# Other column offsets for the first four K tiles, the gated tiles and the down weights in a hybrid decoder layer

## The chip, the cores and the metric

The kernel runs on one core of one Trainium2 chip. Times are device microseconds (us) of one execution; a kernel's time is the median of its runs. TensorE does the matrix products, ScalarE and VectorE split and evict, GpSimd does small sums, SyncE issues the weight transfers.

## What is computed

One decoder layer on 256 tokens and 16 meta tokens, width 2048, in fp32: the input projection, sparse attention over a shared latent for half of the width, multi-scale pooling for the other half, then

```python
mix = jnp.concatenate([attn_out, pool_out], axis=-1) @ w_o[l]
h = layer_norm(ALPHA * h + mix, ln1_g[l], ln1_b[l])
z = h @ w_up                      # (272, 2048) @ (2048, 11264)
z = depthwise causal convolution of width 3 over z, plus a bias
a, g = jnp.split(z, 2, axis=-1)
f = (jax.nn.gelu(a) * g) @ w_down # (272, 5632) @ (5632, 2048)
h = layer_norm(ALPHA * h + f, ln2_g[l], ln2_b[l])
```

## The kernel before

Every fp32 number is split in two parts of type fp32r, an upper part (ScalarE, L170 for weights) and the rest (VectorE, L171), and a product of two numbers is three matmuls: upper by upper, and the two mixed ones. So one K tile (128 of the 2048 rows that are summed over) is a triple of matmuls. `product` (L268) runs 16 such triples into one PSUM bank: the first matmul of a triple stands at L275, the other two at L278. In these products a 128x128 block of weights is stationary and the activations, 256 to 272 tokens wide, are the moving operand. `hl.turned` sets the order of the last two: (upper weights, lower activations), then (lower weights, upper activations), or the other way round (turned).

The stages in order of time: the indexer's queries (8 products on `xp`, 256 tokens), keys and values, the attention's queries (8 on `xp`, 258 tokens), the pooling channels with the softmax between (8), the output projection (16 products, `output`, L704, on `mixp` and `mixa`), the first 8 up products on `fold` (260 columns), 80 up products on `hp` (258 tokens), and the down projection. The up products and the down projection alternate weight tile by weight tile (`ffn_plan`): `seven` (L862) computes 2x2 blocks with seven products; there the gated activations (`gp`, `right`) are stationary and the weights are the moving operand, 512 wide, in triples at L873 to L875. L925 to L927 and L1079 to L1081 are down products of the last two parts in the plain form.

Nothing is computed from where a tile lies, but the kernel sets it carefully. `weight_tiles` gives each weight tile 4224 words per partition; `places` (L106) returns the offset of the upper and of the lower part in it, whether the order is turned, and with `lead` and `gap` a step in columns: for `UP` the first 512 columns (the first four K tiles) lie at 12 and the others at 12 + 52. `Parts` (L87) places the two parts of an activation tile in its slot of 576 words: `first` and `first + 274`. The slots of the ring and the weight tiles are multiples of 64 words apart (576 and 4224), and the pools put both at 24 words past a multiple of 64. So an operand's place modulo 64 words is the same for every tile of its kind:

| operand (place modulo 64 words) | before | after |
|---|---|---|
| indexer queries: weights, activations | 34, 40 and 58 | the same |
| output projection, first four K tiles: weights, activations | 24, 26 and 44, turned | 34, 40 and 58, not turned |
| output projection, other K tiles | 24, 26 and 44, turned | the same |
| up on `hp`, first four K tiles | 36, 26 and 44, turned | 34, 40 and 58, not turned |
| up on `hp`, other K tiles | 24, 26 and 44, turned | the same |
| up on `fold`, first four K tiles | 36, 24 and 56, turned | 34, 40 and 58, not turned |
| up on `fold`, other K tiles | 24, 24 and 56, turned | 24, 26 and 44, turned |
| `gp` slots, upper and lower part (stationary) | 56 and 24 | 24 and 24 |
| `right`, upper and lower part | 24 and 56 | 24 and 24 |
| split down weights (moving) | 16 | 20 |
| the last part's down weights | 24 (`whl_y`: 24 and 32) | 20 |

K tiles are summed in the order of `K_PROJ`, `K_O` and `K_UP`, in which the weights also lie; the output projection alone took them in another order (`order`, L701) than they lie in. PE's instructions are a fixed list; nothing here reorders it. SyncE's queue fetches the weight tiles in the order of use, two ahead (three buffers).

Of the kernel before, what the change touches and what calls it, by code (L numbers as in the profile page):

```python
# [17 lines left out]
P = 128  # L18
D = 2048
NM = 16  # L20
S = 256
# [62 lines left out]
        return self.tile[rows, o + a:o + b]  # L84


class Parts:  # L87


# [8 lines left out]
WIDE = 288  # L98
QUERY = (10, 10 + 2048, False)
HEAD = (12, 12 + 2048, True)  # L100
OUTPUT = (0, 2048, True)
UP = (12, 12 + 2112, True, 512, 52)
DOWN = (56, 56 + 2048)


def places(n, kind):  # L106
# [4 lines left out]


K_PROJ = (1, 3, 5, 7, 9, 11, 13, 15, 0, 2, 4, 6, 8, 10, 12, 14)
K_O = (1, 3, 5, 7, 9, 10, 12, 14, 0, 2, 4, 6, 8, 11, 13, 15)
K_UP = (1, 3, 5, 7, 8, 10, 12, 15, 0, 2, 4, 6, 9, 11, 13, 14)


# [1 line left out]
def tile_layer(ctx, tc, xt, w_first, w_proj, w_uk, w_uv, w_pool, w_o, w_up, w_down, cols, rows, rel_bias, onehot, out):  # L119
# [82 lines left out]
    def emit(i):  # L202
        if i in ready:
            return
        if i == last:

            raw = wp.tile([P, 2048], F32, tag="wraw", name="wraw")
            nc.sync.dma_start(raw, stream[i])
            raws[i] = raw
            ready[i] = []  # L210
            for c in range(0, 2048, 256):
                hl = ring.tile([P, 2, 258], F32R, tag="act", name="whl_r", padded_shape=[P, 2, WIDE])
                nc.scalar.activation(hl[:, 0, :256], raw[:, c:c + 256], AF.Copy)
                nc.vector.tensor_tensor(hl[:, 1, :256], raw[:, c:c + 256], hl[:, 0, :256].bitcast(F32), op=ALU.subtract)
                ready[i].append(hl)
            return
        if i == spare:
            raw = wp.tile([P, 2048], F32, tag="wraw", name="wraw")
            hl = Split(sb.tile([P, 4160], F32R, tag="y", name="whl_y"), 0, 2056)
        else:  # L220
            raw, hl = weight_tiles((0, 2112) if i > spare else places(i, where.get(i)))
        ready[i] = hl
        if i == VALUES:

            nc.sync.dma_start(raw, stream[i])
# [42 lines left out]
    def product(ps, hl, act, lo, hi, places, ks=None, k0=0, k1=KT):  # L268

        for n in range(k0, k1):  # L270
            k = (places if ks is None else ks)[n]
            w = slice(P * places.index(k), P * places.index(k) + P)
            wh, wl = hl[:, 0, w], hl[:, 1, w]
            ah, al = act[k][:, 0, lo:hi], act[k][:, 1, lo:hi]
            nc.tensor.matmul(ps, wh, ah, start=n == 0, stop=False)  # L275
            turn = ((wl, ah), (wh, al)) if hl.turned else ((wh, al), (wl, ah))
            for i, (a, b) in enumerate(turn):
                nc.tensor.matmul(ps, a, b, start=False, stop=i == 1 and n == KT - 1)  # L278

# [328 lines left out]
    def values(h, pts, ptx):  # L608
        ps = small()
        hs = slice(h * HD, (h + 1) * HD)  # L610
        nc.tensor.matmul(ps[:, :NQ], vs[0][:, hs], ptx, start=True, stop=False)
        nc.tensor.matmul(ps[:, 2:NQ], vs[1][:, hs], pts[:, :2 * P], start=False, stop=False)  # L612
        nc.tensor.matmul(ps[:, 2 + P:NQ], vs[2][:, hs], pts[:, 2 * P:], start=False, stop=True)
        a = Parts(ring.tile([P, 2, WIDE], F32R, tag="act", name="mixa"), 2, NQ)
        nc.scalar.activation(a[:, 0, :NQ], ps[:, :NQ], AF.Copy)
        nc.vector.tensor_tensor(a[:, 1, :NQ], ps[:, :NQ], a[:, 0, :NQ].bitcast(F32), op=ALU.subtract)
        mix[h] = a
# [33 lines left out]
    def pooled(g, df, hl):  # L651
        for j in range(2):
            ps = small()
            for c in range(2):
                w = slice(256 * c + j * P, 256 * c + j * P + P)
                nc.tensor.matmul(ps[:, :NQ], hl[:, 0, w], df[:, c, 0, :], start=c == 0, stop=False)
                nc.tensor.matmul(ps[:, :NQ], hl[:, 0, w], df[:, c, 1, :], start=False, stop=False)
                nc.tensor.matmul(ps[:, :NQ], hl[:, 1, w], df[:, c, 0, :], start=False, stop=c == 1)
            m = 2 * g + j
            a = Parts(ring.tile([P, 2, WIDE], F32R, tag="act", name="mixp"), 2, NQ)  # L660
# [37 lines left out]
        lg = lg_next  # L698


    order = [14, 15, 12, 13, 10, 11, 0, 1, 2, 3, 4, 5, 6, 7, 8, 9]  # L701
    KC = 4

    def output(m):  # L704
        hl = weights()
        ps = big()
        product(ps[:, :NQ], hl, mix, 0, NQ, K_O, ks=order, k1=6 if m == 0 else KT)
        if m == 0:
            values(H - 1, *turned)
            less_token(*mean)  # L710
            product(ps[:, :NQ], hl, mix, 0, NQ, K_O, ks=order, k0=6, k1=14)
            pooled(*late)
            product(ps[:, :NQ], hl, mix, 0, NQ, K_O, ks=order, k0=14)
# [15 lines left out]
    def about_k(m):  # L729
# [57 lines left out]
    def normalise(m):  # L787
# [4 lines left out]
        a = Parts(ring.tile([P, 2, WIDE], F32R, tag="act", name="hp"), 2, NQ)  # L792
# [35 lines left out]
    held = {}  # L828

    def two_parts(a, src):  # L830
        nc.scalar.activation(a[:, 0], src, AF.Copy)
        nc.vector.tensor_tensor(a[:, 1], src, a[:, 0].bitcast(F32), op=ALU.subtract)
        return a

    def slot():
        a = fp.tile([P, 2, NE], F32R, name="gp", tag="gp", bufs=16, padded_shape=[P, 2, WIDE])
        return a[:, :, :2 * P].rearrange("p a (b c) -> p a b c", c=P)

    def forms(r, j, whole):
# [9 lines left out]
        right = ring.tile([P, 2, T], F32R, tag="act", name="right", padded_shape=[P, 2, WIDE])  # L851
        right = two_parts(right[:, :, :2 * P].rearrange("p a (b c) -> p a b c", c=P), s[:, 2:])
        if j % 2 == 0:
            held["lone"], held["other"] = slot(), slot() if whole else None
        two_parts(held["lone"][:, :, j % 2], a22)
        if whole:
            two_parts(held["other"][:, :, j % 2], a21)
# [4 lines left out]
    def seven(kind, part, c, j):  # L862
# [7 lines left out]
        for name, w in names:  # L870
            a, i = pairs[part][j][name]
            ps, w = held[name], slice(512 * w, 512 * w + 512)
            nc.tensor.matmul(ps, a[:, 0, i], hl[:, 0, w], start=j == 0, stop=False)  # L873
            nc.tensor.matmul(ps, a[:, 0, i], hl[:, 1, w], start=False, stop=False)  # L874
            nc.tensor.matmul(ps, a[:, 1, i], hl[:, 0, w], start=False, stop=j == n - 1)  # L875
# [31 lines left out]
    for item in plan:  # L907
# [3 lines left out]
        if item[0] == "down":  # L911
# [9 lines left out]
            for k in range(4 * g, 4 * g + 4):  # L921
                w = slice(512 * (k - 4 * g), 512 * (k - 4 * g) + 512)
                for i in range(2):
                    a, r = pairs[part][k // 2][f"a{i + 1}{k % 2 + 1}"]
                    nc.tensor.matmul(downs[i], a[:, 0, r], hl[:, 0, w], start=k == 0, stop=False)  # L925
                    nc.tensor.matmul(downs[i], a[:, 0, r], hl[:, 1, w], start=False, stop=False)
                    nc.tensor.matmul(downs[i], a[:, 1, r], hl[:, 0, w], start=False, stop=k == n - 1)  # L927
            if g == n // 4 - 1:
                for i in range(2):
                    yc = y2[:, i, 512 * c:512 * c + 512]  # L930
# [43 lines left out]
                continue  # L974
        gate(*both)
        if part > FAST:
            a = fp.tile([P, 2, NE], F32R, name="gp", tag="gp", bufs=16, padded_shape=[P, 2, WIDE])
            gated.append(two_parts(a[:, :, :S], both[0]))
        elif f % 2:
            todo.append((part, pair))  # L980

# [90 lines left out]
    for i in range(2):  # L1072
        t, mv = slice(i * P, (i + 1) * P), mvs[i]
        waiting = []
        for q, (a, b) in enumerate(cuts[i]):
            ps = small() if i else big()
            for j, k in enumerate(order):
                for o, wh, wl in pieces(hls[k], a, b):
                    nc.tensor.matmul(ps[:, o], gated[k][:, 0, t], wh, start=j == 0, stop=False)  # L1079
                    nc.tensor.matmul(ps[:, o], gated[k][:, 0, t], wl, start=False, stop=False)  # L1080
                    nc.tensor.matmul(ps[:, o], gated[k][:, 1, t], wh, start=False, stop=j == n - 1)  # L1081
# [91 lines left out]
```

## Time and profile before

| | |
|---|---|
| median of 3 runs | 1034.46 us (1034.37 to 1036.26) |
| the profiled execution | 1035.45 us, of which the span from the first to the last instruction is 1033.7 us |
| TensorE matmul busy | 1025.6 us, 99% of the span |
| VectorE, ScalarE, GpSimd busy | 86%, 60%, 18% |
| granted TensorE clock | 0.998 |

A row of a timeline gives the start in us, the length, the engine, the line, the operation, out<-in, the shape and how many instructions were merged. A matmul's length covers its way through the array, so neighbours overlap; what one costs is the distance to the next start. Since L275 begins every triple, the distance between two L275 starts is the price of one K tile.

### The profile page before, as it was taken

What the parts mean: (1) busy time and instruction counts of PE and PEld (TensorE: products, weight loads), DVE (VectorE), ACT (ScalarE), POOL (GpSimd) and SP (SyncE); (2) the same over time, 40 slices, a digit from 0 to 9 for tenths busy, and PEclk for the clock granted to TensorE, in tenths of its full rate; (3) what the DMA queues carried; (4) which work ended last, traced back from release to release, by engine and by line L of the source; (5) the groups of instructions that cost most, each with busy time, mean ns of one, the idle gap of its engine ahead of it and who ended that gap; (6) DMA issues with size and microseconds to landing.
All of it is one profiled execution on the core that took longest, in us unless ns stands there. A gap on an engine that the chain in (4) does not pass through costs nothing.

```text
span 1033.7 us, 19199 instructions
## 1 busy us (share of the span) xinstructions
PE 1025.6 (99%) x7644; PEld 976.8 (94%) x7644; DVE 890.8 (86%) x1401; ACT 621.1 (60%) x1000; POOL 185.4 (18%) x245
## 2 busy tenths in 40 slices
PE   9999999999999999999999999999999999999997
PEld 8999999999999999999999999999999999999986
DVE  6878668758879998998999999989999999999876
ACT  6656346645549855565666556565556565566675
POOL 1200014125430021120121101211112111120031
PEclk9999999999999999999999999999999999999999
DMA  9655643454554578978887788887978779887874
GB/s 328 243 187 210 226 154 106 145 194 168 200 196 137 194 225 242 287 281 288 291 277 266 277 296 275 269 277 266 300 264 286 270 278 288 277 276 274 289 235 142
DMA packets 59754, 250.28 MB, mean 242 GB/s; under 512 B 21734, under 2 KB 22416, under 8 KB 32656
## 3 DMA queue, kind: packets, MB, share of 16 engines
q1 hardware_dynamic: 34592, 230.42, 62.1%
q0 software_dynamic: 7888, 16.14, 8.2%
q10 hardware_dynamic: 17184, 2.49, 1.5%
q8 instruction: 60, 0.98, 0.4%
q14 instruction: 30, 0.25, 0.1%
HBM read 232.50 MB, written 2.11 MB: 227 GB/s over the span
## 4 chain that ended last, share of the span: by engine, by line
PE 94%; issue 2%; DVE 1%; DMA 1%; POOL 1%; ACT 0%; POOLq 0%; SPq 0%; DVEq 0%; ACTq 0%
PE mm L278 47%; PE mm L275 24%; PE at L873 6%; PE at L875 6%; PE at L874 6%; PE mm L349 2%; DMA wraw<-in_w_down 1%; DVE whl L171 1%; PE mm L577 0%; PE at L438 0%; PE at L612 0%; PE at L439 0%; POOL gb L992 0%; DMA wraw<-in_w_first 0%; PE at L324 0%
## 5 line engine op out<-in xcount | busy, mean ns | idle before, releaser
L171 DVE TENSOR_TENSOR whl<-wraw,whl 128x1024 fp32r<-128x1024 f32 (+1 forms) x416 | 486.5, 1204 | 37.0 <-ACT whl L170 36.0
L170 ACT ACTIVATE whl<-wraw 128x1024 fp32r<-128x1024 f32 (+1 forms) x416 | 402.7, 1015 | 99.3 <-DVE wraw L182 20.6
L278 PE MATMUL mm<-hp,whl 128*128 128x258 f32 x2560 | 459.6, 281 | 0.0
L278 PEld LDWEIGHTS mm<-hp,whl 128*128 128x128 f32 x2560 | 395.5, 189 | 3.1
L275 PE MATMUL mm<-hp,whl 128*128 128x258 f32 x1280 | 362.2, 283 | 0.0
L275 PEld LDWEIGHTS mm<-hp,whl 128*128 128x128 f32 x1280 | 240.4, 188 | 3.2
L278 PE MATMUL mm<-xp,whl 128*128 128x256 f32 (+5 forms) x768 | 140.2, 282 | 0.0
L278 PEld LDWEIGHTS mm<-xp,whl 128*128 128x128 f32 x768 | 118.7, 189 | 0.5
L275 PE MATMUL mm<-xp,whl 128*128 128x256 f32 (+5 forms) x384 | 112.0, 292 | 0.0
L808 ACT ACTIVATE z<-mm,cv 128x256 f32<-128x256 f32 x40 | 22.6, 564 | 97.7 <-PE mm L278 97.7
L845 POOL TENSOR_TENSOR forms<-za 128x128 f32<-128x128 f32 x20 | 21.2, 1062 | 307.1 <-DVE za L826 240.5
L275 PEld LDWEIGHTS mm<-xp,whl 128*128 128x128 f32 x384 | 72.2, 188 | 1.0 <-issue 0.5
L875 PE MATMUL at<-whl,gp 128*128 128x512 f32 x180 | 70.7, 394 | 0.0
L874 PE MATMUL at<-whl,gp 128*128 128x512 f32 x180 | 70.7, 394 | 0.0
L873 PE MATMUL at<-whl,gp 128*128 128x512 f32 x180 | 69.4, 395 | 0.0
L808 ACT ACTIVATE za<-mm,cv 128x256 f32<-128x256 f32 x40 | 22.6, 564 | 75.6 <-PE mm L278 67.9
L848 POOL TENSOR_TENSOR forms<-za 128x128 f32<-128x128 f32 x20 | 20.3, 1014 | 199.8 <-DVE za L826 199.8
L278 PE MATMUL mm<-fold,whl 128*128 128x260 f32 x256 | 46.3, 283 | 0.0
L278 PE MATMUL mm<-mixp,whl 128*128 128x258 f32 x256 | 45.4, 278 | 0.0
L278 PE MATMUL mm<-mixa,whl 128*128 128x258 f32 x256 | 45.2, 278 | 0.0
L875 PEld LDWEIGHTS at<-whl,gp 128*128 128x128 f32 x180 | 33.8, 188 | 8.1
L874 PEld LDWEIGHTS at<-whl,gp 128*128 128x128 f32 x180 | 33.9, 188 | 6.8
(339 smaller groups left out, 1607.8 us busy)
## 6 DMA issues: line engine op xcount, KB each, us to landing
wraw<-in_w_up SPq DMA_DIRECT2D x88, 1024.0 KB, 5.0
wraw<-in_w_down SPq DMA_DIRECT2D x80, 1024.0 KB, 6.3
wraw<-in_w_proj SPq DMA_DIRECT2D x24, 1024.0 KB, 5.4
wraw<-in_w_o SPq DMA_DIRECT2D x16, 1024.0 KB, 4.9
y<-v POOLq DMA_DIRECT2D x27, 256.0 KB, 8.5
y<-u POOLq DMA_DIRECT2D x18, 256.0 KB, 4.9
wraw<-in_w_first SPq DMA_DIRECT2D x8, 304.0 KB, 5.4
x<-in_xt SPq DMA_DIRECT2D x1, 2176.0 KB, 8.0
```

The costliest lines, as they stand in the source:

```text
L170: upper = nc.scalar.activation(hl[:, 0, c], like(raw[:, c], hl, c), AF.Copy)
L171: lower = nc.vector.tensor_tensor(hl[:, 1, c], like(raw[:, c], hl, c), hl[:, 0, c].bitcast(F32), op=ALU.subtract)
L275: nc.tensor.matmul(ps, wh, ah, start=n == 0, stop=False)
L278: nc.tensor.matmul(ps, a, b, start=False, stop=i == 1 and n == KT - 1)
L349: nc.tensor.matmul(ps[:m, :T], hl[:, t // 2, a0 + a:a0 + a + m], x_parts[k][:, t % 2, :], start=k == 0 and t == 0, stop=k == KT - 1 and t ...
L808: nc.scalar.activation(z, src[:, 2:NQ], AF.Identity, bias=col(C_B, j), scale=col(C_W, 3 * j + 2))
L845: nc.gpsimd.tensor_tensor(s[:, 0], a21, a22, op=ALU.add)
L848: nc.gpsimd.tensor_tensor(s[:, 3], a11, a21, op=ALU.subtract)
L873: nc.tensor.matmul(ps, a[:, 0, i], hl[:, 0, w], start=j == 0, stop=False)
L874: nc.tensor.matmul(ps, a[:, 0, i], hl[:, 1, w], start=False, stop=False)
L875: nc.tensor.matmul(ps, a[:, 1, i], hl[:, 0, w], start=False, stop=j == n - 1)
```

## The change

The first four K tiles of the output and up products get the places of the indexer's queries, both weights and activations, and their order is no longer turned. The output projection's weights lie in the order of use. The parts of the gated tiles lie 320 words apart instead of 288 and their pool begins 32 words later; the down weights begin 4 words later. The number of instructions and their shapes stay, but for the splits of the output projection's weights, whose 1024-column pieces are now written with a step after 512 columns in their first half, as those of the up weights are.

```diff
+def begin(k, places):
+    return 2 + 14 * (places.index(k) < 4)
...
-OUTPUT = (0, 2048, True)
-UP = (12, 12 + 2112, True, 512, 52)
-DOWN = (56, 56 + 2048)
+OUTPUT = UP = (10, 10 + 2112, True, 512, 54)
+DOWN = (60, 60 + 2048)
...
-K_O = (1, 3, 5, 7, 9, 10, 12, 14, 0, 2, 4, 6, 8, 11, 13, 15)
+K_O = (14, 15, 12, 13, 10, 11, 0, 1, 2, 3, 4, 5, 6, 7, 8, 9)
...
-            hl = Split(sb.tile([P, 4160], F32R, tag="y", name="whl_y"), 0, 2056)
+            hl = Split(sb.tile([P, 4352], F32R, tag="y", name="whl_y"), 60, 60 + 2112)
-            raw, hl = weight_tiles((0, 2112) if i > spare else places(i, where.get(i)))
+            raw, hl = weight_tiles((60, 60 + 2112) if i > spare else places(i, where.get(i)))
...
-            turn = ((wl, ah), (wh, al)) if hl.turned else ((wh, al), (wl, ah))
+            turn = ((wl, ah), (wh, al)) if hl.turned and w.start >= hl.lead else ((wh, al), (wl, ah))
...
-        a = Parts(ring.tile([P, 2, WIDE], F32R, tag="act", name="mixa"), 2, NQ)
+        a = Parts(ring.tile([P, 2, WIDE], F32R, tag="act", name="mixa"), begin(h, K_O), NQ)
...
-    order = [14, 15, 12, 13, 10, 11, 0, 1, 2, 3, 4, 5, 6, 7, 8, 9]
-        product(ps[:, :NQ], hl, mix, 0, NQ, K_O, ks=order, k1=6 if m == 0 else KT)
+        product(ps[:, :NQ], hl, mix, 0, NQ, K_O, k1=6 if m == 0 else KT)
...
-    acc = fp.tile([P, NQ], F32, name="acc", tag="acc", bufs=1, padded_shape=[P, 4 * P])
+    acc = fp.tile([P, NQ], F32, name="acc", tag="acc", bufs=1, padded_shape=[P, 4 * P + 32])
...
-        a = fp.tile([P, 2, NE], F32R, name="fold", tag="gp", bufs=16, padded_shape=[P, 2, WIDE])
+        a = Parts(fp.tile([P, 2, WIDE], F32R, name="fold", tag="gp", bufs=16), begin(m, K_UP), NE)
...
+    def halves(a):
+        flat = a.rearrange("p a b -> p (a b)")
+        return [flat[:, c:c + 2 * P].rearrange("p (b c) -> p b c", c=P) for c in (0, 2 * WIDE - 2 * P)]
+
     def slot():
-        a = fp.tile([P, 2, NE], F32R, name="gp", tag="gp", bufs=16, padded_shape=[P, 2, WIDE])
-        return a[:, :, :2 * P].rearrange("p a (b c) -> p a b c", c=P)
+        return halves(fp.tile([P, 2, WIDE], F32R, name="gp", tag="gp", bufs=16))
```

`mixp` and `hp` get `begin` in the same way, `right` and the last part's gated tiles get `halves`, and the matmuls of the down projection index the parts as `a[0]` and `a[1]`.

## Rows read from the trace of the kernel before

**Rows 1.** The page: the span, the busy engines, the chain of waits by engine
```profile
span 1033.7 us, 19199 instructions
PE 1025.6 (99%) x7644; PEld 976.8 (94%) x7644; DVE 890.8 (86%) x1401; ACT 621.1 (60%) x1000; POOL 185.4 (18%) x245
PE 94%; issue 2%; DVE 1%; DMA 1%; POOL 1%; ACT 0%; POOLq 0%; SPq 0%; DVEq 0%; ACTq 0%
```

**Rows 2.** Windows by stage: us, PE, PEld, DVE, ACT, POOL busy, PEclk, DMA share, GB/s
```profile
212.00:299.00 87.00, 87.00 (x750) 86.88 (x749) 65.53 (x79) 44.02 (x79) 36.83 (x48) 1.00 0.53 183
400.00:979.00 579.00, 579.00 (x4157) 545.50 (x4156) 531.47 (x728) 345.84 (x483) 90.35 (x106) 1.00 0.83 279
```

**Rows 3.** Groups of instructions, PE, by form: busy us, mean ns, idle before
```profile
L278 PE MATMUL mm<-hp,whl 128*128 128x258 f32 x2560 | 459.6, 281 | 0.0
L275 PE MATMUL mm<-hp,whl 128*128 128x258 f32 x1280 | 362.2, 283 | 0.0
```

**Rows 4.** Timeline, PE: an up product on hp, of the slower kind
```profile
499.81 0.28 PE L275 MATMUL mm<-hp,whl 128*128 128x258 f32 x1
...
501.24 0.28 PE L275 MATMUL mm<-hp,whl 128*128 128x258 f32 x1
...
501.59 0.29 PE L275 MATMUL mm<-hp,whl 128*128 128x258 f32 x1
...
504.89 0.29 PE L275 MATMUL mm<-hp,whl 128*128 128x258 f32 x1
```

**Rows 5.** Timeline, PE: the next up product on hp, of the faster kind
```profile
507.72 0.28 PE L275 MATMUL mm<-hp,whl 128*128 128x258 f32 x1
...
509.16 0.28 PE L275 MATMUL mm<-hp,whl 128*128 128x258 f32 x1
...
512.63 0.28 PE L275 MATMUL mm<-hp,whl 128*128 128x258 f32 x1
```

**Rows 6.** Timeline, PE: an up product on hp, of the middle kind
```profile
361.07 0.28 PE L275 MATMUL mm<-hp,whl 128*128 128x258 f32 x1
...
362.84 0.28 PE L275 MATMUL mm<-hp,whl 128*128 128x258 f32 x1
```

**Rows 7.** Timeline, PE: the output projection, two neighbouring products
```profile
260.00 0.28 PE L275 MATMUL mm<-mixp,whl 128*128 128x258 f32 x1
...
265.54 0.28 PE L275 MATMUL mm<-mixp,whl 128*128 128x258 f32 x1
```

**Rows 8.** Timeline, PE: an indexer query product, 256 tokens
```profile
46.28 0.28 PE L275 MATMUL mm<-xp,whl 128*128 128x256 f32 x1
...
48.40 0.28 PE L275 MATMUL mm<-xp,whl 128*128 128x256 f32 x1
```

**Rows 9.** Timeline, PE: an up product on fold, 260 columns
```profile
332.03 0.28 PE L275 MATMUL mm<-fold,whl 128*128 128x260 f32 x1
...
333.83 0.28 PE L275 MATMUL mm<-fold,whl 128*128 128x260 f32 x1
```

**Rows 10.** Timeline, PE: 512-wide down matmuls, weights at 16; then at 24
```profile
980.06 0.40 PE L926 MATMUL mm<-whl,gp 128*128 128x512 f32 x1
...
982.39 0.39 PE L927 MATMUL mm<-whl,gp 128*128 128x512 f32 x1
...
1003.63 0.39 PE L1079 MATMUL mm<-whl,gp 128*128 128x512 f32 x1
...
1005.01 0.40 PE L1079 MATMUL mm<-whl_y,gp 128*128 128x512 f32 x1
...
1005.48 0.40 PE L1081 MATMUL mm<-whl_y,gp 128*128 128x512 f32 x1
```

**Rows 11.** Groups by form, ACT: splits in 212 to 299 us, then in 400 to 979 us
```profile
L170 ACT ACTIVATE whl<-wraw 128x1024 fp32r<-128x1024 f32 x30 | 31.0, 1053 | 32.7 <-PE mm L278 18.5 <-issue 14.1
L170 ACT ACTIVATE whl<-wraw 128x1024 fp32r<-128x1024 f32 x249 | 251.1, 1052 | 57.7 <-DVE wraw L182 20.6 <-DMA wraw<-in_w_up 19.6 <-DVE wraw L187 12.3
```

**Rows 12.** Waits of PE, longest first, whole span: us in total, times, longest
```profile
PE at L1063 <- ACT diag L1061: 1.5, 1, 1.5
```

More of the change, by code (lines that the diff above doesn't have):

```diff
@@ L659, in pooled @@
             m = 2 * g + j
-            a = Parts(ring.tile([P, 2, WIDE], F32R, tag="act", name="mixp"), 2, NQ)
+            a = Parts(ring.tile([P, 2, WIDE], F32R, tag="act", name="mixp"), begin(8 + m, K_O), NQ)
             nc.scalar.activation(a[:, 0, :NQ], ps[:, :NQ], AF.Copy, scale=col(G_POOL, m))
@@ L710, in output @@
             less_token(*mean)
-            product(ps[:, :NQ], hl, mix, 0, NQ, K_O, ks=order, k0=6, k1=14)
+            product(ps[:, :NQ], hl, mix, 0, NQ, K_O, k0=6, k1=14)
             pooled(*late)
-            product(ps[:, :NQ], hl, mix, 0, NQ, K_O, ks=order, k0=14)
+            product(ps[:, :NQ], hl, mix, 0, NQ, K_O, k0=14)
         yd = y[:, m, Q0:]
@@ L791, in normalise @@
         nc.scalar.activation(yd, yd, AF.Identity, bias=col(LN1, 2 * m + 1), scale=col(LN1, 2 * m))
-        a = Parts(ring.tile([P, 2, WIDE], F32R, tag="act", name="hp"), 2, NQ)
+        a = Parts(ring.tile([P, 2, WIDE], F32R, tag="act", name="hp"), begin(m, K_UP), NQ)
         nc.scalar.activation(a[:, 0, :NQ], yd, AF.Copy)
@@ L830, in two_parts @@
     def two_parts(a, src):
-        nc.scalar.activation(a[:, 0], src, AF.Copy)
-        nc.vector.tensor_tensor(a[:, 1], src, a[:, 0].bitcast(F32), op=ALU.subtract)
-        return a
+        nc.scalar.activation(a[0], src, AF.Copy)
+        nc.vector.tensor_tensor(a[1], src, a[0].bitcast(F32), op=ALU.subtract)
+        return a
+    def halves(a):
+        flat = a.rearrange("p a b -> p (a b)")
+        return [flat[:, c:c + 2 * P].rearrange("p (b c) -> p b c", c=P) for c in (0, 2 * WIDE - 2 * P)]
     def slot():
-        a = fp.tile([P, 2, NE], F32R, name="gp", tag="gp", bufs=16, padded_shape=[P, 2, WIDE])
-        return a[:, :, :2 * P].rearrange("p a (b c) -> p a b c", c=P)
+        return halves(fp.tile([P, 2, WIDE], F32R, name="gp", tag="gp", bufs=16))
     def forms(r, j, whole):
@@ L850, in forms @@
         mid = two_parts(slot(), s[:, :2])
-        right = ring.tile([P, 2, T], F32R, tag="act", name="right", padded_shape=[P, 2, WIDE])
-        right = two_parts(right[:, :, :2 * P].rearrange("p a (b c) -> p a b c", c=P), s[:, 2:])
+        right = two_parts(halves(ring.tile([P, 2, WIDE], F32R, tag="act", name="right")), s[:, 2:])
         if j % 2 == 0:
             held["lone"], held["other"] = slot(), slot() if whole else None
-        two_parts(held["lone"][:, :, j % 2], a22)
+        two_parts([a[:, j % 2] for a in held["lone"]], a22)
         if whole:
-            two_parts(held["other"][:, :, j % 2], a21)
+            two_parts([a[:, j % 2] for a in held["other"]], a21)
         return {"P1": (left, 0), "P2": (left, 1), "P5": (mid, 0), "P3": (mid, 1), "P6": (right, 0),
@@ L872, in seven @@
             ps, w = held[name], slice(512 * w, 512 * w + 512)
-            nc.tensor.matmul(ps, a[:, 0, i], hl[:, 0, w], start=j == 0, stop=False)
-            nc.tensor.matmul(ps, a[:, 0, i], hl[:, 1, w], start=False, stop=False)
-            nc.tensor.matmul(ps, a[:, 1, i], hl[:, 0, w], start=False, stop=j == n - 1)
+            nc.tensor.matmul(ps, a[0][:, i], hl[:, 0, w], start=j == 0, stop=False)
+            nc.tensor.matmul(ps, a[0][:, i], hl[:, 1, w], start=False, stop=False)
+            nc.tensor.matmul(ps, a[1][:, i], hl[:, 0, w], start=False, stop=j == n - 1)
         if j < n - 1:
@@ L924, in tile_layer @@
                     a, r = pairs[part][k // 2][f"a{i + 1}{k % 2 + 1}"]
-                    nc.tensor.matmul(downs[i], a[:, 0, r], hl[:, 0, w], start=k == 0, stop=False)
-                    nc.tensor.matmul(downs[i], a[:, 0, r], hl[:, 1, w], start=False, stop=False)
-                    nc.tensor.matmul(downs[i], a[:, 1, r], hl[:, 0, w], start=False, stop=k == n - 1)
+                    nc.tensor.matmul(downs[i], a[0][:, r], hl[:, 0, w], start=k == 0, stop=False)
+                    nc.tensor.matmul(downs[i], a[0][:, r], hl[:, 1, w], start=False, stop=False)
+                    nc.tensor.matmul(downs[i], a[1][:, r], hl[:, 0, w], start=False, stop=k == n - 1)
             if g == n // 4 - 1:
@@ L976, in tile_layer @@
         if part > FAST:
-            a = fp.tile([P, 2, NE], F32R, name="gp", tag="gp", bufs=16, padded_shape=[P, 2, WIDE])
-            gated.append(two_parts(a[:, :, :S], both[0]))
+            a = slot()
+            two_parts([t.rearrange("p b c -> p (b c)") for t in a], both[0])
+            gated.append(a)
         elif f % 2:
@@ L1078, in tile_layer @@
                 for o, wh, wl in pieces(hls[k], a, b):
-                    nc.tensor.matmul(ps[:, o], gated[k][:, 0, t], wh, start=j == 0, stop=False)
-                    nc.tensor.matmul(ps[:, o], gated[k][:, 0, t], wl, start=False, stop=False)
-                    nc.tensor.matmul(ps[:, o], gated[k][:, 1, t], wh, start=False, stop=j == n - 1)
+                    nc.tensor.matmul(ps[:, o], gated[k][0][:, i], wh, start=j == 0, stop=False)
+                    nc.tensor.matmul(ps[:, o], gated[k][0][:, i], wl, start=False, stop=False)
+                    nc.tensor.matmul(ps[:, o], gated[k][1][:, i], wh, start=False, stop=j == n - 1)
             yc = y2[:, i, a:min(b, 2048)]
```

## The prediction

> **What bounds the kernel now.** I read the page first: TensorE has a matmul in the array for 1025.6 of 1033.7 us, and 94% of the chain of waits is TensorE's own work [rows 1]. The waits of PE name 1.5 us as the longest wait for another engine in the whole span [rows 12]. So the time is the sum over TensorE's list of instructions of what each costs, and a change that leaves the list alone can only act through that price. A busy share of 99% does not say that the price is the lowest: a matmul's length of 281 to 283 ns is its way through the array [rows 3], and the price is the distance to the next start, which only the timeline gives. The granted clock is 1.00 in the stages of rows 2, the level of 2.4 GHz; 258 columns are 0.1075 us at that clock, three of them 0.3225 us.
>
> Now the reader should compare equal work. The output projection does one K tile in 5.54/16 = 0.346 us [rows 7]. An up product on hp has the same shapes, and in its last twelve K tiles the same places modulo 64 words and the same order. Yet one such product goes on at (504.89 - 501.59)/9 = 0.367 us per K tile [rows 4], the next at (512.63 - 509.16)/10 = 0.347 [rows 5], and a third kind at 1.77/5 = 0.354 [rows 6]. By the starts at L275 in the timeline, 38 of the 80 products on hp keep the pace of rows 4 to their end, 39 that of rows 5 and 3 that of rows 6; from 400 us on slow and fast alternate without exception. The fast and the slow product run the same instructions on operands at the same places. What differs is how they enter: their first four K tiles take about the same time (501.24 - 499.81 = 1.43 us against 509.16 - 507.72 = 1.44), but with another spacing inside, and after them a pace is fixed. So the pace depends on the places and on the moment at which a series begins; the first four K tiles are a run-up. That the output products, whose sixteen K tiles all have one place, are fast throughout fits: nothing disturbs them.
>
> **The change part by part**, summed against the profiled execution (1035.45 us, 1.0 above the median of 1034.46); I apply the differences to the median.
>
> 1. *Up products on hp.* No instruction is added. The run-up gets the places and order of the indexer's queries. Their pace is (48.40 - 46.28)/6 = 0.353 us per K tile with 256 tokens [rows 8]; two more columns in three matmuls add 0.0025 at 2.4 GHz: 0.356, so four cost 1.42 us, as now (1.43, 1.44): 0. What counts is the pace afterwards. Between the two products the 14 K tiles from the first start to the last shown take 5.08 and 4.91 us, a difference of 0.17, and two more tiles add 2 x 0.02: 0.21 us per product [rows 4, 5]. Bounds: all 38 products at 0.367 go to 0.347, -38 x 0.21 = -8.0, and the three middle ones -3 x 12 x 0.007 = -0.25; or all 39 at 0.347 go to 0.367, +8.2, with +0.45 for the middle ones. No row shows the new run-up with 258 columns in front of these places. The queries repeat one spacing from tile to tile, which speaks for one and the same moment at the end of every run-up. But with 256 columns, not 258. I take half of the gain, -4.0: slow and fast alternate now, so that there are two ways of entering, and one of them may come to hit the fast pace every time while the other goes on missing it every other time.
>
> 2. *Output projection.* Now always fast [rows 7]. The run-up at 0.356 instead of 0.346 costs 4 x 0.01 x 16 = +0.6 us. What follows can lose the fast pace: 12 x 0.0205 = 0.245 per product, 3.9 us for all sixteen. It cannot gain, for no row is below 0.346. I take four of the sixteen products at 0.367: +1.0.
>
> 3. *Up products on fold.* Now 1.80/5 = 0.360 per K tile with 260 columns [rows 9]. Their places become those of hp. With the fast pace, 4 x 0.3585 + 12 x 0.3495 = 5.63 us against 5.76, -0.13 x 8 = -1.1; with the slow one +0.9. I take -0.5.
>
> 4. *Down projection.* 756 matmuls at L873 to L875 and 96 at L925 to L927, all 512 wide, at (982.39 - 980.06)/10 = 0.233 us [rows 10]. The weights go from 16 to 20 and the stationary parts, now at 56 and 24, both to 24. Nearest rows: weights at 24 cost (1005.01 - 1003.63)/6 = 0.230, the tile after them 0.47/2 = 0.235 [rows 10]. So between -852 x 0.003 = -2.6 and +852 x 0.002 = +1.7; I take -0.6, a quarter of the gain, since the ends are about as far from the present price on either side and the row nearest in its places is the lower one.
>
> 5. *Splits.* Their count stays. The output projection's are now written with a step, as the up weights already are: 1053 ns for ScalarE in the output stage and 1052 among the up and down products [rows 11]: 0. Slots begin later by some words, no buffer is added and no transfer or queue is moved; 0. The cover is VectorE: between 400 and 979 us it is busy 531.5 of 579 us [rows 2]. If PE saved all 8 us there, VectorE would still have 40 us to spare, so the splits stay hidden; beyond that they would bound.
>
> 6. *The order of the output weights.* The same K tiles in the same order, now from the first half of a weight tile onwards. The first tiles need only the first split; the stage shows no PE idle (87.00 of 87.00 us, [rows 2]): 0.
>
> Sum: -4.0 - 0.1 + 0.6 + 1.0 - 0.5 - 0.6 = **-3.6 us, 1030.9 us**.
>
> **A rule against this change.** The timeline shows 0.347 and 0.367 us for the same triple [rows 4, 5]. The Trainium skill, "TensorE: Matmul & The Clock Gate", back-to-back issue gap, gives N / 2.4 + 2.5 ns, an estimate of 0.330 us per triple of 258 columns wherever the operands lie; and under "What happens when you issue a matmul" it says that loading the next weights does not steal read bandwidth from the running matmul. By that every place costs the same and the kernel stays at 1034.5 us. This trace does not agree: three paces for one shape, all above the estimate.
>
> **The rivals.**
>
> *All fast.* Every run-up ends at the right moment. For it: the queries' steady spacing [rows 8]; the fast pace holds once taken, over all sixteen output products. Against it: 256 columns, not 258. -8.0 - 0.25 - 1.1 + 0.6 - 0.6 = -9.4: 1025.1 us.
>
> *No change.* Products on hp stay mixed as they are, because how they enter still depends on the down matmuls before them, or because the places work only through the entry and not by themselves: 1034.5, with 2 us to either side for the outputs and the down matmuls.
>
> *The output projection loses its pace.* Mechanism: it has no run-up of other places now [rows 7]; with one, its later K tiles must enter anew sixteen times, as hp's do, and take the pace of rows 4. Price 0.245 us per product and 0.04 for the run-up; if all sixteen fall and hp stays mixed, +3.9 + 0.6 - 0.1 - 0.6 = +3.8: 1038.3 us. It decides, if hp gains nothing, from eight slow output products on.
>
> *All slow.* The new run-up ends always at the moment that leads to 0.367: +8.2 + 0.45 + 4.5 + 0.9 = +14.0: 1048.5 us. For it: two of three known paces are above the fast one, and before 400 us the slow one comes as often as the fast.
>
> **How the numbers follow.** Half of the gain 0.33, all fast 0.15, no change 0.23, outputs slow 0.16, all slow 0.13. About 0.2%, 2.1 us, is what a measurement of this kernel can tell from no change. Faster takes the first two and 0.02 of the mixed case: 0.50. Same: 0.19. Slower: 0.16 + 0.13 + 0.02 = 0.31. The range reaches from all fast, 1025, to 1040, past the case of slow outputs with the dear end of the down matmuls (1038.3 + 0.6 + 1.7); it leaves out all slow and little else. As cases of both signs hold much of the chance, the likeliest one's own range is 1028 to 1033.
>
> **What would show it.** In the timeline of the changed kernel, the starts at L275 (shifted by the new lines) in products on hp: 0.347 after the fourth K tile in more than 39 of 80 if I am right; alternating as now if nothing changed; 0.367 everywhere if all slow. The output products: 0.346 kept or lost from the fifth K tile on. The down matmuls: 0.230 or 0.235. Wrong would be the whole reading if the paces stood as they are and the time moved, or if PE showed new waits for the splits at L170 and L171 in the list of waits.

## The result and the profile after

The changed kernel takes 1040.62 us (four runs, 1040.11 to 1041.00) against 1035.18 for the kernel before, a ratio of 1.0053 with an interval of 1.0037 to 1.0069: slower by 5.4 us, outside the predicted range by 0.6 us and on the other side. In the experiments' runs the kernel before itself took either 1033.6 to 1036.3 us or 1038.4 to 1040.6, from one execution to the next and for a reason that stays open, since no trace of it at the dearer time was taken; this moves the ratios of experiments by up to 0.4%, so the readings below rest on distances between starts in the traces.

The page of the changed kernel (span, busy engines, chain by engine), the answer to [rows 1]:

```profile
span 1038.9 us, 19199 instructions
PE 1031.6 (99%) x7644; PEld 981.5 (94%) x7644; DVE 890.6 (86%) x1401; ACT 620.3 (60%) x1000; POOL 185.3 (18%) x245
PE 96%; issue 2%; DMA 1%; POOL 1%; ACT 0%; SPq 0%; DVE 0%; POOLq 0%; ACTq 0%
```

TensorE's busy time grew by 6.0 us and the span by 5.2; VectorE and ScalarE did the same work. As before, the longest wait of TensorE for another engine is 1.5 us. The granted clock is 1.00 between 400 and 979 us, as before (us, then busy time of PE, PEld, DVE, ACT and POOL, PEclk, DMA share, GB/s):

```profile
400.00:979.00 579.00, 579.00 (x4124) 545.58 (x4123) 529.44 (x727) 343.76 (x483) 90.33 (x107) 1.00 0.83 277
```

So the time lies in the price of the instructions, as the prediction said, and the starts must be read. The lengths hardly tell: in the groups by form the products on hp [rows 3] grew by 2.6 and 0.7 us in sum.

```profile
L282 PE MATMUL mm<-hp,whl 128*128 128x258 f32 x2560 | 462.2, 281 | 0.0
L279 PE MATMUL mm<-hp,whl 128*128 128x258 f32 x1280 | 362.9, 284 | 0.0
```

The timeline (start, length, engine, line) of the changed kernel, a product on hp behind twelve wide matmuls (the 512-wide ones of the down projection) and the next one, behind nine. L279 begins every K tile, as L275 did before:

```profile
490.61 0.39 PE L879 MATMUL at<-whl,gp 128*128 128x512 f32 x1
...
493.19 0.40 PE L881 MATMUL at<-whl,gp 128*128 128x512 f32 x1
493.43 0.28 PE L279 MATMUL mm<-hp,whl 128*128 128x258 f32 x1
...
494.87 0.28 PE L279 MATMUL mm<-hp,whl 128*128 128x258 f32 x1
...
496.30 0.28 PE L279 MATMUL mm<-hp,whl 128*128 128x258 f32 x1
...
498.73 0.28 PE L279 MATMUL mm<-hp,whl 128*128 128x258 f32 x1
...
499.08 0.39 PE L879 MATMUL at<-whl,right 128*128 128x512 f32 x1
...
500.24 0.40 PE L881 MATMUL at<-whl,right 128*128 128x512 f32 x1
500.47 0.40 PE L879 MATMUL at<-whl,gp 128*128 128x512 f32 x1
500.71 0.40 PE L880 MATMUL at<-whl,gp 128*128 128x512 f32 x1
500.95 0.40 PE L881 MATMUL at<-whl,gp 128*128 128x512 f32 x1
501.18 0.28 PE L279 MATMUL mm<-hp,whl 128*128 128x258 f32 x1
...
502.62 0.28 PE L279 MATMUL mm<-hp,whl 128*128 128x258 f32 x1
...
506.65 0.29 PE L279 MATMUL mm<-hp,whl 128*128 128x258 f32 x1
```

Three things are to be seen. The first four K tiles take 1.44 us in both, as in [rows 4, 5]. Behind twelve wide matmuls the product comes to the pace of rows 5, 2.43/7 = 0.347 us, but only from the ninth K tile (496.30) on. Behind nine it goes on at 4.03/11 = 0.366, the pace of rows 4. This holds without exception: counted by the starts, all 33 products behind twelve are fast and all 34 behind nine are slow. A down tile with four of the seven block products gives twelve wide matmuls and one with the other three nine, and they come four by four, so the pattern is four fast, four slow, where before it was one by one. Over all 80 products: 43 fast, 37 slow (before 39, 38 and 3 of the middle kind).

The wide matmuls themselves settled. Behind the first few of each group their starts stand 239 and 234 ns apart in turn, whatever product went ahead (the sum of such a pair shows in 500.24, 500.71: 0.47). So after an even number the next product starts at one moment of this alternation and after an odd number at the other. Before, no such alternation of two stands in the starts; from 440 us on the last distance of a group is 225 or 226 ns ahead of a slow product and 230 to 232 ahead of a fast one, with nine or twelve alike. (Distances in whole ns are from the trace's own times, of which the rows show two digits.)

An output product, two neighbours, and ten wide matmuls of the plain form (L931 to L933), the answers to [rows 7] and [rows 10]:

```profile
261.43 0.28 PE L279 MATMUL mm<-mixp,whl 128*128 128x258 f32 x1
...
267.05 0.28 PE L279 MATMUL mm<-mixp,whl 128*128 128x258 f32 x1
...
989.77 0.40 PE L931 MATMUL mm<-whl,gp 128*128 128x512 f32 x1
...
992.14 0.40 PE L932 MATMUL mm<-whl,gp 128*128 128x512 f32 x1
```

This output product costs 5.62 us, 0.07 to 0.08 more than before, all of it in the first K tiles; the fast pace follows, as in thirteen others (the first two of the sixteen miss it). A plain wide matmul costs 2.37/10 = 0.237 in place of 0.233. Summing the distances from start to start, kind by kind, over both traces:

| term | predicted | measured |
|---|---|---|
| products on hp | -4.1 | +2.3 |
| output projection (+0.6 run-up, +1.0 lost pace) | +1.6 | +1.5 |
| products on fold | -0.5 | +0.3 |
| wide matmuls | -0.6 | +1.8 |
| sum | -3.6 | +5.9 |

What lies behind the start of the last matmul is 0.7 us shorter, and the other matmuls differ by 0.1 in sum, which leaves the growth of the span.

### The profile page after: what moved, and what is told of

Read it like the earlier page. It is cut to its first block, busy times and chain, and to the rows that moved or that the text cites. A ratio compares the mean times of both kernels' runs of the same rounds, so it can differ in the third digit from the quotient of the medians.

```text
span 1038.9 us, 19199 instructions
## 1 busy us (share of the span) xinstructions
PE 1031.6 (99%) x7644; PEld 981.5 (94%) x7644; DVE 890.6 (86%) x1401; ACT 620.3 (60%) x1000; POOL 185.3 (18%) x245
## 4 chain that ended last, share of the span: by engine, by line
PE 96%; issue 2%; DMA 1%; POOL 1%; ACT 0%; SPq 0%; DVE 0%; POOLq 0%; ACTq 0%
PE mm L282 47%; PE mm L279 24%; PE at L879 6%; PE at L880 6%; PE at L881 6%; DMA wraw<-in_w_first 1%; PE mm L353 1%; PE mm L932 1%; PE mm L933 1%; PE mm L931 1%; POOL gb L999 0%; PE mm L581 0%; PE at L442 0%; PE at L616 0%; PE at L443 0%
## 5 line engine op out<-in xcount | busy, mean ns | idle before, releaser
L279 PE MATMUL mm<-hp,whl 128*128 128x258 f32 x1280 | 362.9, 284 | 0.0
L279 PEld LDWEIGHTS mm<-hp,whl 128*128 128x128 f32 x1280 | 240.7, 188 | 3.4
L279 PE MATMUL mm<-xp,whl 128*128 128x256 f32 (+5 forms) x384 | 112.0, 292 | 0.0
L279 PEld LDWEIGHTS mm<-xp,whl 128*128 128x128 f32 x384 | 72.3, 188 | 1.0 <-issue 0.5
```

## The experiments

Theory A: a product's pace is set by the moment at which it starts, and the wide matmuls in front set that moment. Theory B: the places alone set it. "Fast" and "slow" below are products on hp that end at 0.347 or at 0.367 us per K tile, by the starts in each trace; where the two don't make up 80, the rest has the middle pace. Prices of wide matmuls are mean distances of starts, over the 882 of them on gated tiles (30 belong to the last part), times 852, against 198.3 us before and 200.1 after. A time is the median of a kernel's executions, while counts and prices come from its one profiled execution; where the two times lie more than 1 us apart, both are given, and the counts explain the second alone.

**One part at a time.** First the run-up of the products on hp alone, on the kernel before:

```diff
+UP_HP = (10, 10 + 2112, True, 512, 54)
...
-        a = Parts(ring.tile([P, 2, WIDE], F32R, tag="act", name="hp"), 2, NQ)
+        a = Parts(ring.tile([P, 2, WIDE], F32R, tag="act", name="hp"), begin(m, K_UP), NQ)
...
```

> The kernel before with one part of the change: the run-up (first four K tiles) of the 72 up products on hp that alternate with the down matmuls and of the 8 before them gets the places and the order of the indexer's queries; outputs, fold, gated tiles and down weights stay. Theory A (the wide matmuls in front set the moment at which a product starts, and the moment fixes its pace): with the old places of the wide matmuls the pattern by fours, slow behind nine wide matmuls and fast behind twelve, does not come back; some other pattern does, and each fast product costs about 0.05 us more than the old fast one for its longer run-up. If half are slow: +1 to +3 us. Theory B (the new run-up itself decides): the same 43 fast and 37 slow products, by fours, as in the changed kernel, and +2.3 us, the difference of the products on hp between the two traces.

Measured: 1047.16 us (profiled execution 1043.72), ratio 1.0088 (1.0056 to 1.0121); 70 slow, 10 fast, all 67 behind nine or twelve slow. One behind nine, with its first, seventh and sixteenth K tile; the last nine distances take 3.30 us, 0.367 each:

```profile
499.77 0.39 PE L881 MATMUL at<-whl,gp 128*128 128x512 f32 x1
500.00 0.28 PE L281 MATMUL mm<-hp,whl 128*128 128x258 f32 x1
...
502.17 0.29 PE L281 MATMUL mm<-hp,whl 128*128 128x258 f32 x1
...
505.47 0.29 PE L281 MATMUL mm<-hp,whl 128*128 128x258 f32 x1
```

The places of a product on hp are those of the changed kernel, the pattern is not: theory B falls. The size was off as well: nobody expected nearly all to be slow.

Then the output projection alone:

```diff
-OUTPUT = (0, 2048, True)
+OUTPUT = (10, 10 + 2112, True, 512, 54)
...
-K_O = (1, 3, 5, 7, 9, 10, 12, 14, 0, 2, 4, 6, 8, 11, 13, 15)
+K_O = (14, 15, 12, 13, 10, 11, 0, 1, 2, 3, 4, 5, 6, 7, 8, 9)
...
```

> The kernel before with one part of the change: the output projection's first four K tiles at the places of the indexer's queries, its weights in the order of use, its first matmuls not turned. Both theories: its sixteen products cost 1.2 to 1.5 us more, since only the run-up is dearer, by 0.09 us per product in the trace of the changed kernel, and fourteen of sixteen keep the fast pace; products on hp and the 512-wide matmuls as before. A rival: the outputs also set the moment at which the up products start, and the number of slow products on hp moves by more than five, 1 us either way.

Measured: 1035.38 us, ratio 0.9987 (0.9971 to 1.0004); the outputs cost 1.2 us more by their starts, the products on hp stay at 38 slow (40 fast, 2 of the middle kind), the wide ones at their price. The interval of the ratio is wider than so small a term; the starts show it. The term is a dearer run-up, and it hardly reaches further than the outputs themselves (products on hp -0.05 us in sum).

Then the places of the wide matmuls, both together, and each alone:

```diff
-DOWN = (56, 56 + 2048)
+DOWN = (60, 60 + 2048)
...
-        return a[:, :, :2 * P].rearrange("p a (b c) -> p a b c", c=P)
+        return halves(fp.tile([P, 2, WIDE], F32R, name="gp", tag="gp", bufs=16))
...
```

> The kernel before with one part of the change: both parts of the gated tiles at 24 and the down weights at 20 modulo 64 words; the run-ups stay (only the two parts of the fold tiles change places with each other, since their pool begins 32 words later). Both theories: the 852 wide matmuls cost 1.7 to 2.0 us more, as in the changed kernel. Theory A: the wide matmuls settle into their alternation of 239 and 234 ns, so products on hp no longer alternate one by one; their pace goes with twelve or nine wide matmuls in front, by fours, or becomes one pace for all. Theory B: with the old run-up they alternate one by one as before, 38 slow, and the total is +1.9 us.

> The kernel before with the gated tiles alone at 24 and 24 modulo 64 words; the down weights stay at 16 and the last part's at 24 (the fold tiles have their two parts exchanged as in the earlier run). In the run with both, all products on hp were slow and the 672 wide matmuls of the gated slots cost 2.6 us more. If the gated places do it: the same here, 70 slow products and +2 to +3 us in the wide matmuls. If the down weights do it: the wide matmuls at their old 232.5 ns, and the slow and fast products alternate as before or in a new pattern.

> The kernel before with the down weights alone at 20 modulo 64 words (the last part's too); the gated tiles stay at 56 and 24. The gated tiles alone left the wide matmuls within 0.3 us of their price; both together cost 1.8 to 2.6 us. If the down weights carry that price: the 672 wide matmuls of the gated slots cost 1.5 to 2.6 us more, their alternation of 239 and 234 ns is there. If only the two together do: at most 0.5 us more. The products on hp: a new pattern in either case; if they stay slow and fast one by one, the time is 1035 to 1037 us, if nearly all are slow, 1043.

| changed | time, us | profiled execution, us | ratio | slow of 80 | wide matmuls, us |
|---|---|---|---|---|---|
| both | 1048.57 | 1043.72 | 1.0109 (1.0074 to 1.0145) | 70 | 200.9 (+2.6) |
| gated tiles alone | 1043.09 | 1041.70 | 1.0071 (1.0044 to 1.0097) | 73 | 198.7 (+0.4) |
| down weights alone | 1040.56 | 1040.10 | 1.0060 (1.0045 to 1.0075) | 74 | 196.9 (-1.4) |

In none of the three was a place of a product on hp touched (with the gated tiles the two parts of the fold tiles exchange places), and in all of them the products on hp turned slow: theory A again. The parts don't add up: the run-up alone and the wide places alone have spans of 1041.9 us each, 8.3 above the kernel before, and the whole change 1038.9. The price of the wide matmuls is no sum of two parts: the down weights at 20 make them cheaper, until the gated tiles stand at 24 and 24. Ten plain ones in a row, first with the gated tiles alone changed, then with the down weights alone:

```profile
986.18 0.40 PE L933 MATMUL mm<-whl,gp 128*128 128x512 f32 x1
...
988.52 0.40 PE L934 MATMUL mm<-whl,gp 128*128 128x512 f32 x1
```

```profile
984.64 0.39 PE L925 MATMUL mm<-whl,gp 128*128 128x512 f32 x1
...
986.94 0.40 PE L926 MATMUL mm<-whl,gp 128*128 128x512 f32 x1
```

These are 0.234 and 0.230, against 0.233 before and 0.237 with both. So the expectation that the down weights carry the price fell; only the two together do.

**Moving the moment alone.** The sharpest test leaves all places as in the changed kernel and gives only the first matmul of a product more columns, so that all later ones start that much later.

```diff
-            nc.tensor.matmul(ps, wh, ah, start=n == 0, stop=False)
+            if n == 0 and more:
+                nc.tensor.matmul(more[0][:, :hi + more[1]], wh, act[k][:, 0, lo:hi + more[1]], start=True, stop=False)
+            else:
+                nc.tensor.matmul(ps, wh, ah, start=n == 0, stop=False)
...
```

> The changed kernel with eight more columns in one matmul, the first one of each product on hp that stands behind nine wide matmuls (36 products): 266 columns in place of 258, so that all that follows starts 8 columns later; the eight results are not used. In the trace of the changed kernel these products start their second matmul some 8 columns of 2.4 GHz earlier, counted modulo 16, than those behind twelve. Theory A: they take the fast pace, 36 x (0.187 - 0.003) = -6.6 us against the changed kernel, about 1034 us, and some 79 of 80 products are fast. Theory B: the pace hangs on places alone: they stay slow, and the time goes up by 36 x 8 columns, 0.1 us.

Measured: 1039.81 us; the pattern by fours stayed, 37 slow. My way of counting the moment (second starts modulo 16 columns) was wrong, or eight was one of the widths that don't help. So all even widths went through one kernel:

> The changed kernel with 2, 4, ... 14 more columns in the first matmul of every product on hp behind wide matmuls, in turn, counted apart for those behind twelve and those behind nine (results not used). Eight columns behind nine did not turn them fast. Theory A (the moment decides): some of the seven widths turn the products behind nine fast and others turn those behind twelve slow, and which does is the same in all five repetitions. Theory B: the pattern by fours stays through all widths, 37 slow.

Measured (one run, 1040.89 us), by the products of each width, fast (F) or slow (S); products of one width never parted:

| columns in the first matmul | 258 | 260 | 262 | 264 | 266 | 268 | 270 | 272 |
|---|---|---|---|---|---|---|---|---|
| behind twelve | F | F | F | S | S | S | S | F |
| behind nine | S | F | S | S | S | F | S | S |

The column of 258 is the changed kernel. Two neighbours in this timeline, both behind nine, with 266 and 268 columns:

```profile
581.98 0.28 PE L281 MATMUL mm<-hp,whl 128*128 128x266 f32 x1
...
583.43 0.28 PE L283 MATMUL mm<-hp,whl 128*128 128x258 f32 x1
...
587.45 0.29 PE L283 MATMUL mm<-hp,whl 128*128 128x258 f32 x1
...
589.93 0.28 PE L281 MATMUL mm<-hp,whl 128*128 128x268 f32 x1
...
591.38 0.28 PE L283 MATMUL mm<-hp,whl 128*128 128x258 f32 x1
...
595.20 0.28 PE L283 MATMUL mm<-hp,whl 128*128 128x258 f32 x1
```

The last eleven K tiles take 4.02 us with 266 columns and 3.82 with 268, on the same places and in the same order. The other hand on the same lever, a tenth wide matmul behind the nine:

```diff
...
+                nc.tensor.matmul(ps[:, :n], tenth[0], tenth[1][:, :n], start=True, stop=True)
             product(ps[:, :NQ], hl, h_parts, 0, NQ, K_UP, ks=late_last if f == FOLDED else None)
```

> The changed kernel with a tenth wide matmul, its result not used, between the nine and the product on hp behind them; its width goes through 256, 260, 264, 268, 320, 384 and 512 columns from product to product (39 products, five or six of each). Theory A' (what counts is whether an even or an odd number of wide matmuls stands in front, since they alternate between 239 and 234 ns): behind 512 columns the product is fast, as behind twelve; of the narrower ones some are fast and some slow. Theory B: all stay slow whatever stands in front. Either way the tenth matmuls cost 107 to 235 ns each, so that the whole is 4 to 6 us dearer if all stay slow and about 1 us cheaper if all turn fast.

Measured (one run, 1042.28 us): from 450 us on, 512 columns and 268 columns always led to a fast product (five each), 256, 260, 264, 320 and 384 always to a slow one (23 in all). Ten matmuls of full width, an even number, do what the theory asks; that ten with a last one of 268 columns do it too shows that the even number is not all that counts. Now the width that was fast on both sides, everywhere:

> The changed kernel with two more columns (260, results not used) in the first matmul of every product on hp behind wide matmuls. In the run with changing widths all ten products with 260 columns were fast, behind twelve and behind nine. Theory A (the moment a series starts decides, and the wide matmuls set it): all products on hp behind wide matmuls are fast, 36 or 37 x 0.187 = -6.8 us against the changed kernel, + 72 x 0.001: about 1034 us, level with the kernel before, since outputs and wide matmuls stay dearer by 3.3 us and each fast product by 0.05 us. A rival (the outcome in the earlier run hung on the neighbours of other widths): the pattern by fours or a mix stays, 1038 to 1041 us.

Measured: 1031.27 us, ratio 0.9968 (0.9955 to 0.9981); 79 of 80 fast. The same products as at 501.18 above, in this kernel:

```profile
498.85 0.40 PE L887 MATMUL at<-whl,gp 128*128 128x512 f32 x1
499.08 0.28 PE L281 MATMUL mm<-hp,whl 128*128 128x260 f32 x1
...
502.30 0.28 PE L283 MATMUL mm<-hp,whl 128*128 128x258 f32 x1
...
504.38 0.28 PE L283 MATMUL mm<-hp,whl 128*128 128x258 f32 x1
```

2.08/6 = 0.347, behind nine. Two columns of one matmul in 48, in the 71 products behind wide matmuls, took 9.4 us off the changed kernel. That is 2.6 us more than expected: the products behind twelve, fast already, gained too, from 5.537 to 5.497 us from first to last start, since they reach the fast pace sooner; those behind nine went from 5.717 to 5.532.

**No run-up.** The other question is what the run-up of the kernel before was worth.

```diff
-UP = (12, 12 + 2112, True, 512, 52)
+UP = (0, 2112, True)
```

> The kernel before with no run-up on the up products: all sixteen K tiles of the up weights at 24 modulo 64 words, as in the output projection. If it is the run-up that makes slow products, all become fast: 38 x 0.216 = -8.2 us. If the wide matmuls in front make them, the products on hp go on as a mix or all slow: between 0 and +8.5 us. The outputs and the 512-wide matmuls as before.

Measured: 1026.65 us, ratio 0.9925 (0.9901 to 0.9948), the best version of the study: 73 of 80 fast. Its page and a product behind nine:

```profile
span 1024.8 us, 19199 instructions
PE 1017.1 (99%) x7644; PEld 966.4 (94%) x7644; DVE 889.7 (87%) x1401; ACT 621.7 (61%) x1000; POOL 185.9 (18%) x245
```

```profile
505.56 0.40 PE L875 MATMUL at<-whl,gp 128*128 128x512 f32 x1
505.80 0.28 PE L275 MATMUL mm<-hp,whl 128*128 128x258 f32 x1
506.16 0.28 PE L275 MATMUL mm<-hp,whl 128*128 128x258 f32 x1
...
511.02 0.28 PE L275 MATMUL mm<-hp,whl 128*128 128x258 f32 x1
```

The fast pace holds almost from the second K tile, 4.86/14 = 0.347. It is tempting to read this as "uniform places are fast". The next run has the same products on hp and the new places of the wide matmuls:

> The kernel before with no run-up on the up products, and with the changed places of the gated tiles and the down weights. Without a run-up and with the old wide places 73 of 80 products on hp were fast (1026.65 us). Theory A (run-up and wide matmuls decide together): the wide matmuls settle into 239 and 234 ns again, so products behind nine and behind twelve may part, all of one kind fast and all of the other slow, or all one; the wide ones are 2 to 3 us dearer than before, so 1029 us if all are fast, 1036 if half. A rival (a run-up of other places is what makes products slow, whatever stands in front): 70 or more fast, 1028 to 1030 us.

Measured: 1044.88 us, ratio 1.0118 (1.0082 to 1.0153); 67 slow, which are all those behind nine and all behind twelve. The fifth and the sixteenth K tile of one behind nine, 4.03/11 = 0.366:

```profile
500.69 0.29 PE L280 MATMUL mm<-hp,whl 128*128 128x258 f32 x1
...
504.72 0.29 PE L280 MATMUL mm<-hp,whl 128*128 128x258 f32 x1
```

So the absence of a run-up is not what makes products fast either. Last, the two columns on the kernel before, with its own places (the edit is that of the run with two columns):

> The kernel before with two more columns (260, results not used) in the first matmul of every product on hp behind wide matmuls; all places as before. With the changed places the two columns made 79 of 80 products fast. Theory A (the moment a series starts decides, and which moments are good hangs on the run-up and on the wide matmuls): the one-by-one alternation ends, because every product starts two columns later; what takes its place can't be said from the runs so far: 1026.5 us if all are fast, 1043 if all are slow. Theory C (two more columns are good in themselves): 70 or more fast, 1026 to 1028 us. Theory B (places alone): the alternation stays, 1034.5 us.

Measured: 1045.09 us (profiled execution 1043.43), ratio 1.0059 (1.0040 to 1.0077); 71 slow. A product behind nine, its first, sixth and sixteenth K tile, 3.66/10 = 0.366:

```profile
501.13 0.28 PE L277 MATMUL mm<-hp,whl 128*128 128x260 f32 x1
...
502.92 0.29 PE L279 MATMUL mm<-hp,whl 128*128 128x258 f32 x1
...
506.58 0.29 PE L279 MATMUL mm<-hp,whl 128*128 128x258 f32 x1
```

Theory C and theory B fall; the alternation one by one is gone, as theory A has it.

## Why the prediction was wrong

*What bounds the kernel* was right: no new wait, all of the change in prices from start to start, and the pace "depends on the places and on the moment at which a series begins". Two of its readings are too smooth: "from 400 us on slow and fast alternate without exception" holds from 434 us on, for the three products that begin at 409, 418 and 426 us are all fast; and the first of the sixteen output products, in which other matmuls stand, goes on at 0.353 behind them. By its own sign, the paces standing as they are while the time moves, the whole reading came near to being wrong: 37 slow products in place of 38, and 5.4 us more. What holds of it is that the time is in the starts; what it missed is that the way to a pace has a price too.

*Step 1 failed.* It took "half of the gain, -4.0", because "one of them may come to hit the fast pace every time while the other goes on missing it every other time". The wide matmuls' new places gave just two ways of entering, one always fast and one always slow; that is half of the products again, 37 slow in place of 38. The number gave 0.4 us, and two prices that the step had at nothing took 2.7: the 43 fast products cost 47 ns more each (5.480 to 5.527 us from first to last start), the 37 others 19 ns. Only 7 to 12 ns of that lie in the four tiles of the run-up, whose price was estimated well; the rest is the way from there to the steady pace, which behind twelve is reached at the ninth K tile rather than about the fifth, and which the step left out. Of the 9.5 us between the sums of the table, 6.4 lie in this step. The sign that it named for being right, more than 39 fast products, even came: the count said nothing of the price of the way. The error behind it is the sentence on the run-up, "after them a pace is fixed": the run-up does not fix it, as 70 slow products with the new run-up and the old wide matmuls show. That the steady spacing of the queries means "one and the same moment at the end of every run-up" fell with it: behind nine and behind twelve the new run-up takes the same 1.44 us and ends in two paces.

*Step 2* had the sum nearly right by two errors that offset each other. The run-up was put at +0.6 and costs 0.07 to 0.08 us per product, 1.0 us for the last fourteen. The lost pace was put at four products and 1.0 us; the first two products lost it (+0.16 and +0.24 us), the first of them with other matmuls in its middle. From the third on all are fast.

*Step 3* took a gain of 0.5; the fold products kept a mixed pace and cost 0.3 more, inside its bounds. (The table of places gives the parts of a fold tile before as 24 and 56; by its row on the gated tiles, in whose slots they lie, the upper part stands at 56 and the lower at 24.)

*Step 4* took -0.6 within -2.6 and +1.7; it was +1.8. Its bounds came from rows in which one of the two operands stood elsewhere, and the two together do what neither does alone (+0.4, -1.4, and +2.6 for both on the kernel before). A price of a pair of places is not bounded by rows of other pairs. It also took the wide matmuls for a term of their own, when their larger effect is on the products behind them: the three runs that changed only them were slower by 0.6 to 1.1%.

*Steps 5 and 6* held: same splits, no new wait.

*The rivals.* "No change" had the right reason, that "how they enter still depends on the down matmuls before them", and 0.23; its 1036.5 at the dear end is 4 us too low because it took prices as they are. That the output projection loses its pace did not happen. "All slow" did not happen in the changed kernel, but it is what six of the experiments ran into.

*The rule against the change.* The runs show a triple of 258 columns at 0.347 to 0.367 us on equal places. The Trainium skill, "TensorE: Matmul & The Clock Gate", "Back-to-back issue gap", gives N / 2.4 + 2.5 ns, for an isolated matmul as it says, and has no term for places in it. The estimate from that formula, 0.330 us per triple, is below every triple of 258 columns that the traces have in these products (0.345 at the least). By that rule the kernel would have stayed at 1034.5 us; the traces disagree, with the new prices above.

What was not shown: which property of a moment makes it good, and why a run-up and the wide matmuls in front combine as they do. The table of widths is a record of it, not an explanation.

## What to carry to other kernels

Where a matmul's price depends on how its series is entered, a change of places is a change of every entry behind it: count the paces in the trace after each change, product by product, and look for what stands in front of the dear ones. Before searching for better places, move the entry alone, by a few columns in one matmul or by leaving a run-up out; here two columns were worth 9 us on one set of places, and the same two columns cost 8 us on another (spans of 1038.9 and 1029.4 us, 1033.7 and 1041.7), so no setting carries over without its neighbours. A result that needs such luck should be timed again after any edit near it.

## What the runs showed of the hardware

Where a series settles, its pace is a whole multiple of one length. Averaged over the last K tiles, the three paces per K tile are 346.7, 353.3 and 366.7 ns, and a settled pair of wide matmuls takes 473.3: 52, 53, 55 and 71 times 6.67 ns, which is 16 periods of 2.4 GHz. Why, no run shows, and not every series settles: on fold the distances go on changing between 356 and 371 ns. The granted clock was 1.00 in the stages compared, before and after.

A product's pace is a state that holds: once steady, no product's pace changed before its end in any of the traces, and equal entries gave equal paces, 33 of 33 and 34 of 34. The next entry ends it, and wide matmuls are not needed for that. The first nine products on hp of the kernel before follow each other without any, and they go slow, fast, middle, three times over. From the eighth to the sixteenth K tile of the first two it is 2.94/8 = 0.367 and 2.77/8 = 0.346 us; the third is that of [rows 6]:

```profile
350.06 0.29 PE L275 MATMUL mm<-hp,whl 128*128 128x258 f32 x1
...
353.00 0.29 PE L275 MATMUL mm<-hp,whl 128*128 128x258 f32 x1
...
355.83 0.28 PE L275 MATMUL mm<-hp,whl 128*128 128x258 f32 x1
...
358.60 0.28 PE L275 MATMUL mm<-hp,whl 128*128 128x258 f32 x1
```

So theory A names only one thing that sets the moment: there the product in front and the old run-up do. With the new run-up the nine go slow once, then fast eight times.
